# A two-layer streaming encoder on one core: the list scheduler runs twice, the second time by latest start

## The chip, the cores and the metric

The kernel runs on one core of one Trainium2 chip. The metric is device time in microseconds, the median of several executions. One execution was profiled, and every duration below is from it.

## What is computed

Two layers run over 544 frames: 512 of a new stream ("prompt") and 32 of a running one ("sample"), which also reads a cache of 512 past frames. All is fp32.

```python
h = rmsnorm(x, g_attn); z = h @ w_in
o_da = rmsnorm((softmax(q1 k1) - lam * softmax(q2 k2)) @ v) * (1 - lam_init)   # 8 heads, two softmaxes each
o_mla = latent_attention(...)                                                  # 8 heads, one softmax each
x = x + (sigmoid(gA) * o_da + sigmoid(gB) * o_mla) @ w_o
u = rmsnorm(x, g_ffn) @ w_up                                                   # 5632 columns
x = x + (silu(conv3(u)[:2816]) * conv3(u)[2816:]) @ w_down
y = rmsnorm(x, g_final)                                                        # after the second layer
```

Masks are causal by chunks of 64 frames. The outputs are y, the new cache rows and the last two rows of u.

## The kernel before, in words

**Numbers.** Each fp32 operand of a large product is split into a high part (cast to fp32r) and a low part (the rest), and a product is three matmuls: high by high, high by low, low by high. So weights come by DMA into `wf` (a ring of 2), ScalarE casts them into `wh` (ring of 3), and VectorE or GpSimd subtracts to make `wl` (ring of 3). Activations are split alike, into pages of the tile `frt`; plain fp32 pages lie in `fpt`.

**Products.** `dense` runs one block of 128 output columns over all 544 frames: per 128 rows of the weight six matmuls of 272 (or 256 and 288) frames into one of two PSUM slots, `dn`. When a block is done, VectorE evacuates the slot ("evac"). These dense matmuls are most of TensorE's work, and the program always has more of them.

**Side work.** Attention runs beside the dense products. Its score, transpose and value matmuls go into four PSUM banks, `ax`. For one head and one block of 128 queries, a score matmul fills a bank; VectorE masks it (MEMSET) and takes the row maximum (TENSOR_REDUCE `sm<-ax`); ScalarE takes the exponential into `fpt` (`softmax`); VectorE scales (`diff_norm`, `mla_norm`); TensorE transposes the result from `fpt` into an `ax` bank (`probs_t`, matmuls `ax<-ident,fpt`); ScalarE and VectorE split it, and `av` multiplies by the values. Queries and keys are rotated first (`rope_unit`): per unit four DMAs within SBUF (`fpt<-fpt`) swap groups of partitions, and GpSimd multiplies and adds. `split_rows`, `split_twice` and `sk` make high and low parts of queries, keys and cached keys. `finish` joins the two mixers of a pair of heads: per head three long VectorE operations on `fpt` and a split; its result is used only by the output product `w_o`, after all heads. `layer_consts` makes a few small vectors (`lamt`, `bh`, `gdc`).

**The order.** The kernel's code doesn't issue instructions. `Program.add` records each with the earlier ones it depends on (by tile cells, so reuse of a page or bank is a dependency too). `Program.order` then simulates the five engines: again and again it takes the engine that can start first, and on it, among the recorded instructions that are ready, the one recorded earliest. `cost` gives each instruction's time, `SIGNAL` the time from one engine's end to another's start. `emit` issues in that order, and each engine then runs its own instructions strictly in it, whatever the simulated times were. All instructions are issued from one line in `emit`: L371 before.

**Stages.** Each layer: input products with latent attention beside them, then differential attention, gates and `finish`, then `w_o` and the up- and down-products with the convolution. Layer 1 is recorded in the same way as layer 0.

## Time and profile before

| | us |
|---|---|
| median of 3 runs | 1917.09 (1914.59 to 1917.48) |
| the profiled execution, whole | 1917.5 |
| its span, first to last instruction | 1915.7 |
| TensorE busy (PE, matmuls) | 1851.4 |
| VectorE busy (DVE) | 1251.2 |
| ScalarE busy (ACT) | 878.9 |
| GpSimd busy (POOL) | 753.3 |

PE is the matmuls' engine and PEld its weight loads, which overlap; SP issues all DMAs. In the chain of work that ended last, PE has 87% and DVE 8%. A time in a row such as 330.10 is counted from the span's start. DVE instructions that share a port with POOL stretch, so one shape has several durations.

### The profile page before, as it was taken

The numbers are of one execution on the slowest core, as the hardware profiler recorded it, in microseconds if no ns is written. First come the engines' busy times: TensorE is split into PE (matmuls) and PEld (weight loads), VectorE is DVE, ScalarE is ACT, GpSimd is POOL, SyncE is SP. The second block draws the span as 40 slices with busy tenths as digits, with TensorE's granted clock in tenths as the row PEclk, the third lists the DMA queues.
The fourth block names the chain that finished last, engine by engine and source line by source line (L and its number), as shares of the span: only waits on it lengthen the run. The fifth ranks groups of instructions, "written<-read, shape, count | busy, mean of one in ns | idle before, by whom it ended". The sixth has DMA issues, their size and how long they took to land.

```text
span 1915.7 us, 37003 instructions
## 1 busy us (share of the span) xinstructions
PE 1851.4 (97%) x14244; PEld 1814.0 (95%) x14244; DVE 1251.2 (65%) x2457; ACT 878.9 (46%) x1810; POOL 753.3 (39%) x856
## 2 busy tenths in 40 slices
PE   7999999988999999999999999989899999999997
PEld 7999998988999999999999999989889999999997
DVE  6677777798747777742247677687986577777212
ACT  4455564555544444432235454654664444444322
POOL 4422636476243333312233345365653333332121
PEclk9999999999999999999999999999999999999999
DMA  4422433344352222233332225244444533333222
GB/s 154 123 79 79 142 108 117 107 141 125 95 187 88 90 90 89 89 95 117 116 121 92 92 90 157 78 144 116 124 125 128 161 89 89 89 89 88 84 88 77
DMA packets 78824, 208.40 MB, mean 109 GB/s; under 512 B 11132, under 2 KB 13880, under 8 KB 78648
## 3 DMA queue, kind: packets, MB, share of 16 engines
q1 hardware_dynamic: 78648, 206.04, 34.9%
q8 instruction: 112, 1.84, 0.4%
q14 instruction: 64, 0.52, 0.1%
HBM read 170.12 MB, written 23.62 MB: 101 GB/s over the span
## 4 chain that ended last, share of the span: by engine, by line
PE 87%; DVE 8%; issue 2%; DMA 1%; POOL 1%; ACT 1%; SPq 0%; DVEq 0%; ACTq 0%; POOLq 0%
PE dn L371 73%; PE ax L371 13%; DVE fpt L371 3%; DVE frt L371 3%; DVE sm L371 1%; POOL fpt L371 0%; DVE wl L371 0%; DMA fpt<-in_x_dram 0%; SPq L371 0%; ACT frt L371 0%; ACT fpt L371 0%; DVE ax L371 0%; DMA wf<-in_wt_dram 0%; POOL wl L371 0%; DMA fpt<-in_dk_c_dram 0%
## 5 line engine op out<-in xcount | busy, mean ns | idle before, releaser
L371 PE MATMUL dn<-frt,wh 128*128 128x272 f32 (+2 forms) x8032 | 1386.8, 291 | 12.1 <-ACT wh L371 7.2
L371 PEld LDWEIGHTS dn<-frt,wh 128*128 128x128 f32 x8032 | 1157.4, 189 | 22.0 <-ACT wh L371 7.3
L371 PE MATMUL dn<-frt,wl 128*128 128x272 f32 (+2 forms) x4000 | 849.0, 291 | 3.4 <-DVE wl L371 3.4
L371 PEld LDWEIGHTS dn<-frt,wl 128*128 128x128 f32 x4000 | 640.4, 189 | 6.7 <-DVE wl L371 3.6
L371 ACT CAST wh<-wf 128x512 fp32r<-128x512 f32 (+2 forms) x534 | 323.8, 609 | 604.3 <-PE dn L371 511.2
L371 POOL TENSOR_TENSOR wl<-wf,wh 128x512 fp32r<-128x512 f32 x242 | 320.7, 1326 | 553.5 <-ACT wh L371 533.6
L371 DVE TENSOR_TENSOR wl<-wf,wh 128x512 fp32r<-128x512 f32 (+2 forms) x290 | 211.5, 733 | 225.0 <-ACT wh L371 222.7
L371 PE MATMUL ax<-frt 128*128 128x256 f32 (+5 forms) x1164 | 228.3, 323 | 19.5 <-ACT fpt L371 12.9
L371 POOL TENSOR_TENSOR fpt<-fpt 128x544 f32<-128x544 f32 (+1 forms) x144 | 207.8, 1456 | 85.9 <-DMA fpt<-fpt 78.2
L371 DVE TENSOR_TENSOR fpt<-dn,fpt 128x544 f32<-128x544 f32 (+2 forms) x291 | 154.1, 547 | 111.0 <-PE dn L371 97.9
L371 PEld LDWEIGHTS ax<-frt 128*128 128x128 f32 (+1 forms) x1164 | 175.6, 189 | 34.8 <-ACT fpt L371 16.3
L371 DVE SCALAR_TENSOR_TENSOR fpt<-fpt,vec 128x546 f32<-128x546 f32 (+1 forms) x180 | 141.2, 785 | 47.6 <-ACT fpt L371 45.6
L371 ACT ACTIVATE fpt<-ax,sm 128x128 f32<-128x128 f32 (+4 forms) x216 | 112.3, 522 | 65.8 <-DVE sm L371 54.3
L371 ACT CAST frt<-fpt 128x544 fp32r<-128x544 f32 (+5 forms) x166 | 101.7, 622 | 50.3 <-DVE fpt L371 24.1
L371 ACT CAST frt<-ax 128x384 fp32r<-128x384 f32 (+4 forms) x186 | 71.5, 395 | 109.5 <-PE ax L371 108.6
L371 POOL COPY fpt<-cin 128x2 f32<-128x2 f32 x88 | 33.8, 384 | 202.3 <-DVE fpt L371 199.2
L371 DVE TENSOR_TENSOR frt<-fpt,frt 64x544 fp32r<-64x544 f32 (+4 forms) x120 | 99.0, 828 | 13.5 <-ACT frt L371 11.3
L371 DVE TENSOR_TENSOR frt<-ax,frt 128x384 fp32r<-128x384 f32 (+4 forms) x186 | 80.3, 446 | 37.2 <-ACT frt L371 24.7
L371 DVE TENSOR_REDUCE sm<-ax 128x1 f32<-128x128 f32 (+4 forms) x216 | 99.2, 473 | 6.7 <-PE ax L371 5.1
L371 PE MATMUL ax<-ident,fpt 128*128 128x128 f32 (+1 forms) x480 | 82.4, 279 | 18.6 <-DVE fpt L371 16.0
L371 DVE SCALAR_TENSOR_TENSOR frt<-fpt,frt 128x544 fp32r<-128x544 f32 (+1 forms) x76 | 79.1, 1040 | 24.9 <-ACT frt L371 24.0
L371 POOL CAST frt<-frt 64x32 fp32r<-64x32 f32 (+1 forms) x172 | 64.4, 378 | 55.6 <-ACT frt L371 34.6
(88 smaller groups left out, 1192.3 us busy)
## 6 DMA issues: line engine op xcount, KB each, us to landing
wf<-in_wt_dram SPq DMA_DIRECT2D x243, 512.0 KB, 3.6
fpt<-fpt SPq DMA_DIRECT2D x168, 68.0 KB, 2.7
wf<-in_wt_dram SPq DMA_DIRECT2D x16, 384.0 KB, 3.1
fpt<-in_x_dram SPq DMA_DIRECT2D x16, 272.0 KB, 3.6
out_o_dv_dram<-fpt SPq DMA_DIRECT2D x16, 272.0 KB, 2.1
out_o_dk_dram<-fpt SPq DMA_DIRECT2D x16, 272.0 KB, 4.3
xa<-fpt SPq DMA_DIRECT2D x16, 272.0 KB, 2.1
fpt<-xa SPq DMA_DIRECT2D x16, 272.0 KB, 3.6
```

Of the source, the lines that this page charges most:

```text
L371: getattr(getattr(self.nc, eng), name)(*args, **kw)
```

## The change

What is computed, the tiles, the recorded instructions and their dependencies are the same (19734 of them). Three things in the scheduler differ:

- `SIGNAL` and `cost` have other numbers; `MARGIN` (5% on each cost) is gone. `cost` now says too whether an instruction uses the port that DVE and POOL share, and the simulation lets such instructions wait for each other (`port`). `GAP` adds 18 ns behind each instruction of DVE, ACT and POOL.
- DMAs: before, SyncE was held at least 475 ns by each; now 60 ns, and the transfer takes its turn on one shared line (`dma`).
- `order` runs the simulation twice. The first run ranks by the place in the program, as before. `latest` walks that order backwards from the program's end and gives every instruction its latest start: the time at which its first user must start, less signal and cost; TensorE's instructions are also held by the one that follows on TensorE. The second run ranks ready instructions of the other engines by that latest start, and TensorE's still by the place in the program.

```diff
-MARGIN = {"vector": 1.05, "scalar": 1.05, "gpsimd": 1.05}
 SIGNAL = {e: dict(zip(ENGINES, t)) for e, t in (
-    ("tensor", (0, 230, 260, 230, 100)),
-    ("vector", (235, 127, 180, 200, 60)),
-    ("scalar", (240, 140, 0, 210, 60)),
-    ("gpsimd", (190, 90, 90, 104, 60)),
-    ("sync", (0, 0, 0, 0, 0)))}
+    ("tensor", (0, 38, 37, 64, 60)),
+    ("vector", (55, 0, 35, 64, 60)),
+    ("scalar", (100, 33, 0, 78, 60)),
+    ("gpsimd", (55, 34, 33, 0, 60)),
+    ("sync", (60, 60, 60, 60, 60)))}
+GAP = {"tensor": 0.0, "vector": 18.0, "scalar": 18.0, "gpsimd": 18.0}
+PORT_TAIL = {"vector": 100.0, "gpsimd": 150.0}
...
         if eng == "tensor":
-            if name == "transpose" or kw["rhs"].dtype != F32:
-                return max(n, 256) / 2.4 + 2.5, 0.0
-            return 2 * (max(2 * n, 256) / 2.4 + 2.5), 0.0
+            if name == "matmul" and kw["rhs"].dtype == F32:
+                return 2 * max(109.0, 0.907 * n + 1.5), False
+            part = name == "matmul" and kw["lhsT"].ap[0][1] < 128
+            return max(109.0, 0.4535 * n + 1.5) + 190 * part, False
...
+    def latest(self, order):
+
+        late = [0.0] * len(self.ops)
+        need = [0.0] * len(self.ops)
+        chain = 0.0
+        for i in reversed(order):
+            e = self.ops[i][0]
+            t = min(need[i], chain) if e == "tensor" else need[i]
+            late[i] = t = t - self.cost(i)[0]
+            if e == "tensor":
+                chain = t
+            for j in self.deps[i]:
+                f = self.ops[j][0]
+                need[j] = min(need[j], t - (0.0 if e == f and e != "sync" else SIGNAL[f][e]))
+        return late
+
     def order(self):
+        late = self.latest(self.schedule(range(len(self.ops))))
+        return self.schedule([i if op[0] == "tensor" else late[i] for i, op in enumerate(self.ops)])
+
+    def schedule(self, rank):
...
-            i = heapq.heappop(a)
-            hold, lat = self.cost(i)
-            hold *= MARGIN.get(e, 1.0)
-            self.start[i] = t
-            free[e] = t + hold
+            i = heapq.heappop(a)[1]
+            if e == "sync":
+                ap = self.ops[i][2][0]
+                free[e] = t + 60
+                dma = max(t + 1300, dma) + width(ap) * ap.ap[0][1] * 4 / 300.0
+                end = dma + 700
+            else:
+                hold, shared = self.cost(i)
+                end = (max(t, port) if shared else t) + hold
+                if shared:
+                    port = end - PORT_TAIL[e]
+                free[e] = end + GAP[e]
```

All instructions are now issued from L411 instead of L371. Three places show how they moved.

**DVE in the first layer's differential attention, at 319 to 329 us of the profile.** `SCALAR_TENSOR_TENSOR fpt<-fpt` and `fpt<-fpt,gdc` and the split behind them are `finish`; `MEMSET ax` and `TENSOR_REDUCE sm<-ax` are the softmaxes of the next heads. Before:

```order
L371 TENSOR_REDUCE sm<-ax_96 128x1
L371 SCALAR_TENSOR_TENSOR fpt<-fpt 128x544
L371 MEMSET ax_97 64x64
L371 MEMSET ax_95 64x64
L371 SCALAR_TENSOR_TENSOR fpt<-fpt,gdc 128x512
L371 SCALAR_TENSOR_TENSOR fpt<-fpt,gdc,oms 128x32
L371 SCALAR_TENSOR_TENSOR fpt<-fpt 128x544
L371 TENSOR_REDUCE sm<-ax_97 128x1
L371 SCALAR_TENSOR_TENSOR fpt<-fpt,gdc 128x512
L371 TENSOR_TENSOR frt<-fpt,frt 128x544
L371 SCALAR_TENSOR_TENSOR fpt<-fpt,gdc,oms 128x32
L371 MEMSET ax_98 64x64
```

In the changed kernel, from the same softmax on:

```order
L411 TENSOR_REDUCE sm<-ax_96 128x1
L411 MEMSET ax_97 64x64
L411 MEMSET ax_95 64x64
L411 TENSOR_REDUCE sm<-ax_95 128x1
L411 TENSOR_REDUCE sm<-ax_97 128x1
L411 RECIPROCAL rs<-sm 128x1
L411 MEMSET ax_96 64x64
L411 TENSOR_REDUCE sm<-ax_96 128x1
L411 RECIPROCAL sm<-sm 128x1
L411 TENSOR_TENSOR wl<-wf,wh 128x512
L411 TENSOR_TENSOR fpt<-dn_93,fpt 128x544
L411 MEMSET ax_95 64x64
```

The seven instructions of `finish` left this place; the first of them now stand three rows below the last one shown, behind four of the softmaxes' maxima, two weights' low parts and an evacuation.

**DVE a little later, at 408 to 416 us.** `frt<-fpt,frt 64x544` is `split_rows`, `frt<-fpt,frt 128x512` is `sk`, and `fpt<-fpt,sm` is `diff_norm`, whose result TensorE transposes. Before:

```order
L371 MEMSET ax_97 64x64
L371 SCALAR_TENSOR_TENSOR frt<-fpt,frt 64x544
L371 TENSOR_TENSOR frt<-fpt,frt 128x512
L371 RECIPROCAL sm<-sm 128x1
L371 TENSOR_REDUCE sm<-ax_97 128x1
L371 SCALAR_TENSOR_TENSOR sm<-sm,coef 128x1
L371 SCALAR_TENSOR_TENSOR frt<-fpt,frt 64x544
L371 SCALAR_TENSOR_TENSOR fpt<-fpt,sm 128x384
```

In the changed kernel:

```order
L411 RECIPROCAL sm<-sm 128x1
L411 SCALAR_TENSOR_TENSOR sm<-sm,coef 128x1
L411 SCALAR_TENSOR_TENSOR fpt<-fpt,sm 128x384
L411 TENSOR_TENSOR frt<-ax_95,frt 128x128
L411 MEMSET ax_97 64x64
L411 TENSOR_REDUCE sm<-ax_97 128x1
L411 MEMSET ax_96 64x64
L411 TENSOR_REDUCE sm<-ax_96 128x1
L411 TENSOR_TENSOR frt<-fpt,frt 128x512
```

`diff_norm` of 384 columns stood behind both `split_rows` and `sk`; now it stands ahead of all three.

**PE at 328 to 331 us**, where a score matmul of 512 keys (`ax_95<-frt 128x512`) stands among dense ones. Before:

```order
L371 MATMUL ax_97<-frt 128x384 x2
L371 MATMUL dn_93<-frt,wh 128x272 x3
L371 MATMUL dn_93<-frt,wl 128x272 x2
L371 MATMUL dn_94<-frt,wh 128x272 x4
L371 MATMUL dn_94<-frt,wl 128x272 x2
L371 MATMUL dn_94<-frt,wh 128x272 x4
L371 MATMUL dn_94<-frt,wl 128x272 x2
L371 MATMUL dn_94<-frt,wh 128x272 x4
L371 MATMUL dn_94<-frt,wl 128x272 x2
L371 MATMUL dn_94<-frt,wh 128x272 x2
L371 MATMUL ax_95<-frt 128x512 x2
```

In the changed kernel:

```order
L411 MATMUL ax_96<-frt 128x384 x2
L411 MATMUL dn_93<-frt,wl 128x272
L411 MATMUL dn_93<-frt,wh 128x272 x4
L411 MATMUL dn_93<-frt,wl 128x272 x2
L411 MATMUL dn_93<-frt,wh 128x272 x4
L411 MATMUL dn_93<-frt,wl 128x272 x2
L411 MATMUL ax_95<-frt 128x512 x2
L411 MATMUL dn_94<-frt,wh 128x272 x4
L411 MATMUL dn_94<-frt,wl 128x272 x2
L411 MATMUL dn_94<-frt,wh 128x272 x4
L411 MATMUL dn_94<-frt,wl 128x272 x2
```

The matmul of 512 keys now comes ahead of the whole next dense block (`dn_94`) instead of 20 matmuls into it, and the one of 384 keys in `ax_97`, 5 matmuls ahead of that block before, comes 38 matmuls into it. In all, 4427 of TensorE's 14178 recorded instructions stand at another place, 1436 of DVE's 2457, 665 of ACT's 1593, 290 of POOL's 852 and 242 of SyncE's 654.

## Rows read from the trace of the kernel before

**Rows 1.** Page, busy time: us, share of the span, instructions.

```profile
PE 1851.4 (97%) x14244; PEld 1814.0 (95%) x14244; DVE 1251.2 (65%) x2457; ACT 878.9 (46%) x1810; POOL 753.3 (39%) x856
```

**Rows 2.** Windows by stage: stretch, its length, busy us of each engine (instructions), granted clock, DMA.

```profile
0.00:30.00 30.00, 17.93 (x91) 16.29 (x92) 20.12 (x24) 13.97 (x22) 15.59 (x15) 0.92 0.61 192
...
300.00:480.00 180.00, 162.87 (x1219) 155.87 (x1219) 146.25 (x317) 98.21 (x235) 117.81 (x116) 0.99 0.40 124
...
1250.00:1430.00 180.00, 162.54 (x1210) 155.75 (x1210) 150.65 (x330) 100.76 (x248) 112.78 (x113) 0.99 0.43 127
...
1895.00:1916.00 21.00, 9.99 (x74) 9.28 (x72) 7.35 (x20) 2.68 (x6) 4.54 (x6) 0.84 0.30 106
```

**Rows 3.** Waits of PE in 300 to 480 us: us in total, times, longest.

```profile
PE ax L371 <- ACT fpt L371: 7.4, 7, 2.1
PE ax L371 <- DVE fpt L371: 6.9, 5, 3.2
```

**Rows 4.** Chain that ended last: start, us, what; the longest undisturbed dense stretch.

```profile
571.93 392.64 PE dn L371 x3144
```

**Rows 5.** Windows of the first burst and of the stretch behind it.

```profile
320.00:348.00 28.00, 23.11 (x170) 21.31 (x169) 27.75 (x53) 15.94 (x40) 20.86 (x21) 1.00 0.34 97
348.00:380.00 32.00, 32.00 (x241) 30.88 (x241) 21.52 (x64) 17.06 (x44) 9.98 (x9) 1.00 0.32 104
```

**Rows 6.** Timeline of DVE, 320 to 329 us: start, us, instruction.

```profile
320.07 1.87 DVE L371 SCALAR_TENSOR_TENSOR fpt<-fpt 128x544 f32<-128x544 f32 x1 [0.60 <-POOL fpt L371]
...
322.05 0.67 DVE L371 SCALAR_TENSOR_TENSOR fpt<-fpt,gdc 128x512 f32<-128x512 f32 x1
322.65 0.24 DVE L371 SCALAR_TENSOR_TENSOR fpt<-fpt,gdc,oms 128x32 f32<-128x32 f32 x1
322.81 0.71 DVE L371 SCALAR_TENSOR_TENSOR fpt<-fpt 128x544 f32<-128x544 f32 x1
...
323.65 1.55 DVE L371 SCALAR_TENSOR_TENSOR fpt<-fpt,gdc 128x512 f32<-128x512 f32 x1
325.13 1.88 DVE L371 TENSOR_TENSOR frt<-fpt,frt 128x544 fp32r<-128x544 f32 x1
326.93 1.34 DVE L371 SCALAR_TENSOR_TENSOR fpt<-fpt,gdc,oms 128x32 f32<-128x32 f32 x1
...
328.31 0.68 DVE L371 TENSOR_REDUCE sm<-ax 128x1 f32<-128x256 f32 x2
```

**Rows 7.** Timeline of PE: two of its longest waits, in brackets.

```profile
330.10 0.74 PE L371 MATMUL ax<-frt 128*128 128x512 f32 x2 [2.06 <-ACT fpt L371]
...
416.09 0.55 PE L371 MATMUL ax<-ident,fpt 128*128 128x128 f32 x3 [3.20 <-DVE fpt L371]
```

**Rows 8.** Timeline of DVE, 408 to 416 us.

```profile
408.80 1.80 DVE L371 SCALAR_TENSOR_TENSOR frt<-fpt,frt 64x544 fp32r<-64x544 f32 x1
410.63 1.75 DVE L371 TENSOR_TENSOR frt<-fpt,frt 128x512 fp32r<-128x512 f32 x1
...
413.56 1.83 DVE L371 SCALAR_TENSOR_TENSOR frt<-fpt,frt 64x544 fp32r<-64x544 f32 x1
415.42 0.62 DVE L371 SCALAR_TENSOR_TENSOR fpt<-fpt,sm 128x384 f32<-128x384 f32 x1
```

**Rows 9.** Timeline at the start: DVE, and PE's wait for a weight's low part.

```profile
15.81 1.24 DVE L371 TENSOR_TENSOR lamt<-lamv 64x2 f32<-64x2 f32 x1
19.40 1.06 DVE L371 TENSOR_SCALAR bh<-vec 128x16 f32<-128x16 f32 x1
26.52 0.82 PE L371 MATMUL dn<-frt,wl 128*128 128x272 f32 x2 [3.35 <-DVE wl L371]
```

**Rows 10.** Windows behind the waits at 468 to 473 us; the clock is third from the end.

```profile
473.00:475.00 2.00, 2.00 (x9) 1.90 (x10) 1.99 (x8) 1.51 (x5) 1.80 (x4) 0.50 0.05 18
```

**Rows 11.** Timeline of SP: the issue of two shuffles in a row.

```profile
1395.34 1.15 SPq L371 DMA_DIRECT2D fpt<-fpt  x2
```

**Rows 12.** Waits of POOL: us in total, times, longest.

```profile
POOL fpt L371 <- DMA fpt<-fpt: 78.2, 28, 6.2
```

## What the change will do to the time
> **What bounds the kernel now.** I read the page's busy times first: PE is busy 1851.4 of 1915.7 us and no other engine over 65% [rows 1]. So the end is set by the matmuls and by what keeps PE from them, 64.3 us of idle time. The undisturbed stretch in the middle of the chain shows what a dense matmul takes: 392.64 us for 3144, 124.9 ns each [rows 4]. No order can shorten that work; an order can only remove idle time.
>
> The windows by stage say where the idle time is (length less PE's busy time, [rows 2]): 12.1 us in the first 30, of which 7.2 lie before the first matmul; 17.1 in 300 to 480; 17.5 in 1250 to 1430, the same stage of layer 1; and 10.7 behind 1895 (up to the span's end at 1915.7). That leaves 64.3 less 57.4 = 6.9 for the 1500 us between. Two stages of differential attention thus hold 34.6 us.
>
> Next, who PE waits for there: ACT and DVE writing `fpt`, 14.3 of the 17.1 us [rows 3]. ACT's share is the softmax too: a score matmul needs a bank whose exponential has not run, because DVE's maximum for it was late. The windows around the first waits show DVE busy 27.75 of 28 us and, right behind, 21.52 of 32, while PE loses 4.9 us in the first and nothing in the second [rows 5]. DVE has the capacity; its work comes in bursts. The timeline shows what it does in one: from 320.07 to 328.27 stand seven instructions of `finish` [rows 6], whose result nothing uses before `w_o`. The maximum that the bank at 330.10 hangs on comes at 328.31, and PE waits 2.06 us [rows 7]. At 416.09 PE waits 3.20 us for a scaling of 384 columns that began at 415.42 [rows 7, 8]; ahead of it stood three splits of new queries and keys.
>
> **The change part by part.** Nothing is added or removed, so all costs are waits.
>
> *The two attention stages.* In the first burst the seven `finish` instructions, 1.87+0.67+0.24+0.71+1.55+1.88+1.34 = 8.26 us [rows 6], go behind the maxima. The wait they precede is 2.06 us, so it should go whole, though PE's matmul now also stands 20 matmuls earlier, 2.5 us at 124.9 ns: 8.3 less 2.5 still covers 2.06. At 416 the three splits, 1.80+1.75+1.83 = 5.38 us [rows 8], go behind the scaling; its wait is 3.20. Elsewhere the order shows the same picture: at most of PE's longer waits of these stages less DVE work stands ahead of what PE needs, or PE has more dense matmuls ahead of its question (the 384-key scores of the fence on PE come 43 matmuls later, 5.4 us). At a few (six of the 26 longest) neither moved. I take four fifths of 34.6, **28 us**; bounds 0 (DVE's work is conserved) and 34.6.
>
> What does the moved work wait for next? `finish` has until `w_o`. DVE is busy 146.25 of 180 us in the first stage and 150.65 of 180 in the second [rows 2]; shortened by 14 each, that is 88% and 91%: tight but possible.
>
> *The start.* Ahead of the low part that PE awaits for 3.35 us at 26.52, DVE ran `lamt` and `bh`, 1.24+1.06 us [rows 9], which now stand behind it. The low part keeps the sums of squares ahead of it. Of the 4.9 us that PE idles after its first matmul (12.1 less 7.2) I take **3.5**; bounds 0 and 4.9. The 7.2 before it hang on the first loads and stay.
>
> *The other stretches*, 6.9 us [rows 2]. Some waits lose DVE work, but PE's question moved up as well: a third, **2.5**; bounds 0 and 6.9. *The end*: the last instructions keep their order, so 0 of the 10.7.
>
> *The clock.* Behind the waits at 468 to 473 us the granted clock reads 0.50, the 1.2 GHz level [rows 10]; 9 matmuls ran in 2 us instead of 16 at 124.9 ns. The mean clock of each attention stage is 0.99 [rows 2], so falls cost 1% of 180 us in each, 1.8. If PE stops idling before them, they go: 3.6 us at most, 0 at least; I take **2**.
>
> *What the tighter plan costs.* The old table left 230 ns from PE to DVE, the new 38. So in many places PE asks sooner: the 512-key scores, 20 matmuls. Where that meets a late engine, a new wait appears that the trace of before can't show. Going through some twenty such places, PE's question moved up by 5 to 28 matmuls (0.6 to 3.5 us) against a slack of 0.1 to 1.5 us, which bounds new waits by 0 and 17 us. I take **8**, near the middle, since the engines that answer are now often earlier too.
>
> *Sum.* -28 -3.5 -2.5 -2 +8 = -28 us. The profiled execution took 1917.5, so **1889.5**; it is 0.4 above the median of the runs, 1917.09, which is nothing here. A measurement of this kernel can tell some 0.2% (3.8 us) from no change.
>
> **The rivals.**
>
> *DVE stays the bound (0.22).* In a burst DVE is busy all the time [rows 5], and work put off 4 us falls on the next head's. For it: 88 to 91% is a load at which something is nearly always late. Against it: the 32 us behind the burst hold 10.5 idle ones. Then half of the 28 comes back, the clock falls stay: -14-3.5-2.5+8 = -12, **1905.5**. One shape of `finish` took 1.87 us and 0.71 us in the same burst [rows 6], the long one while POOL worked. The Trainium skill (SBUF — State Buffer, "SBUF: two separate sides") says that DVE instructions with two SBUF inputs and GpSimd instructions exclude each other for a whole instruction; the two durations agree. By that rule moved work keeps its collisions, which speaks for this rival.
>
> *The score banks bind (0.10).* Waits that ACT ends are waits for an `ax` bank, 7.4 of 17.1 us in the first stage [rows 3]. If four banks are simply too few, those stay: 28 less 2 x 0.8 x 7.4 = 16; the sum is -16, **1901.5**. The Trainium skill (Perfetto Trace Analysis, "Optimization Strategy") reads bubbles that repeat on the engine that should be saturated as possibly too little SBUF or PSUM for the next tile. The trace agrees that a bank is what is waited for, but shows its reader late behind `finish`.
>
> *SyncE is underpriced: slower (0.10).* The new plan holds SyncE 60 ns per DMA. Two shuffles in a row took 1.15 us [rows 11], so the four of a rotation need 2.3, and the last leaves up to 2.1 us after the plan has it. POOL runs strictly in order; it already waited for shuffles 28 times, 78.2 us [rows 12], and weights' low parts stand behind the rotation on its queue. A layer has 21 rotations. If PE then waits 2.1 us at each of 42, that is 88 us; it breaks even with the gain of 28 at 13 of them. At half of them the time is 1917.5-28+44 = **1933.5**. Against it: PE's waits name POOL's rotations nowhere.
>
> *The new waits equal the old (0.06)*, 1917: both orders keep PE in program order, and two thirds of its instructions stand where they stood.
>
> **How the numbers follow.** The forecast's own case has 0.52: range 1871 (34.6+4.9+6.9 gone and no new wait: 46) to 1902 (new waits of 17, half of the small terms). Faster: 0.52+0.22+0.10 = 0.84, less a little for a weak form of the second, 0.82; slower by SyncE and other new waits 0.11; within 0.2%, 0.07. The range takes in the DVE and bank rivals: 1870 to 1912, leaving out slower and no change (0.18).
>
> **What would show it.** Right: PE's idle time in the two attention stages falls from 17 to some 4 to 8 us each; DVE's 99% windows thin out; `finish` runs in stretches where DVE idled; the clock falls after 400 us vanish. Wrong: PE idle there above 12 us with DVE still over 95% busy beside it (DVE rival), waits ended by ACT as large as before (bank rival), or PE waiting for POOL's low parts behind rotations (SyncE).

## The result, and the profile after

The changed kernel takes **1943.95 us** (median of 4 runs, 1940.44 to 1944.73) against 1917.28 for the kernel before, measured beside it: a ratio of **1.0132**, 95% interval 1.0103 to 1.0161. It is slower by 1.3%, where 1889.5 us had been forecast. Its profiled execution took 1943.76 us, span 1942.0.

First the busy time of PE, from the page, beside [rows 1], and the cores view of the kernel before and of the changed one (span, mean granted clock).

```profile
PE 1872.5 (96%) x14244; PEld 1832.2 (94%) x14244; DVE 1261.2 (65%) x2457; ACT 882.9 (45%) x1810; POOL 773.6 (40%) x856
```

```profile
core 0: 1915.7 us, clock 0.994
```

```profile
core 0: 1942.0 us, clock 0.980
```

The span grew by 26.3 us. Idle time of PE is span less busy: 64.3 us before, 69.5 now, so only 5.2 of the 26.3. The other 21.1 are *busy* time of the same 14244 matmuls. The clock is why: the trace's clock record has 4 stretches at 0.50 (the 1.2 GHz level) that end before PE does in the kernel before, 17.1 us together, and 14 now, 71.7 us. The time from each PE instruction's start to the next one's, less waits, less the median of the same pair of shapes, says the same: inside the stretches at 0.50 the excess is 7.8 us before and 31.7 now, everywhere else 41.9 and 37.6. So the dense matmul is what it was (124.9 ns; the longest undisturbed stretch is again 392.64 us for 3144), and some 24 us are lost at the lower level.

The windows by stage, to be held against [rows 2]:

```profile
0.00:30.00 30.00, 18.47 (x97) 16.78 (x98) 20.50 (x27) 14.27 (x22) 16.93 (x16) 0.84 0.61 195
300.00:480.00 180.00, 167.34 (x1207) 160.31 (x1206) 135.96 (x299) 91.80 (x221) 110.57 (x111) 0.95 0.36 113
1250.00:1430.00 180.00, 167.04 (x1224) 159.49 (x1223) 139.24 (x295) 93.92 (x224) 112.59 (x111) 0.96 0.39 115
```

In these two windows PE idles 12.7 us (17.1 before) and 13.0 (17.5), 8.9 less together. But a window ends at a fixed time, the changed kernel reaches the end of each attention stage later, and its last waits there (0.62, 2.64 and 0.46 us at 483 to 487, and 0.62, 2.64 and 0.71 us at 1437 to 1441) lie outside. Windows that hold the whole stage in both kernels, first before, then changed:

```profile
300.00:490.00 190.00, 172.87 (x1293) 165.65 (x1293) 155.54 (x349) 105.74 (x257) 121.10 (x119) 0.99 0.42 128
1250.00:1445.00 195.00, 177.52 (x1323) 170.19 (x1323) 162.60 (x361) 110.67 (x273) 115.42 (x116) 0.99 0.43 125
```

```profile
300.00:490.00 190.00, 173.62 (x1240) 165.78 (x1239) 145.34 (x317) 97.13 (x235) 116.79 (x117) 0.94 0.37 115
1250.00:1445.00 195.00, 178.08 (x1292) 169.79 (x1291) 153.37 (x326) 101.21 (x244) 121.14 (x120) 0.96 0.40 119
```

Counted so, PE idles 16.4 us (17.1 before) and 16.9 (17.5): 1.3 less, not 8.9. And with *more* busy time it got through *fewer* matmuls (1240 for 1293, 1292 for 1323), at a clock of 0.94 and 0.96 where 0.99 stood. Within the first stage the idle time moved: it grew from 5.3 to 7.1 us between 300 and 365 us and from 3.2 to 3.7 between 460 and 490, and fell from 8.6 to 5.5 in the stretch between.

Behind the stages there are new waits. The timeline of PE at the entry of `w_o`, layer 0, in the changed kernel:

```profile
534.96 0.77 PE L411 MATMUL dn<-frt,wh 128*128 128x272 f32 x4 [3.21 <-ACT frt L411]
536.56 0.82 PE L411 MATMUL dn<-frt,wh 128*128 128x272 f32 x2 [0.83 <-DVE frt L411]
```

The kernel before, at the same matmul:

```profile
524.39 1.28 PE L371 MATMUL dn<-frt,wh 128*128 128x272 f32 x6 [0.23 <-ACT frt L371]
```

Layer 1 repeats it at 1487.83 (3.20) and 1489.43 (0.60). The two entries cost 7.8 us of idle time, six times what the attention stages gained. What the clock does behind such a wait shows in windows of the changed kernel (length; busy us and instructions of PE, PEld, DVE, ACT, POOL; granted clock):

```profile
348.00:355.00 7.00, 5.99 (x27) 5.96 (x28) 6.84 (x10) 2.80 (x7) 3.45 (x4) 0.51 0.34 98
536.00:542.50 6.50, 5.94 (x25) 5.71 (x26) 3.58 (x8) 2.66 (x5) 2.16 (x4) 0.50 0.05 19
```

25 matmuls in 5.94 us of busy time; at 124.9 ns they need 3.1.

**What became of the first burst** [rows 5 to 7]. PE waits there 2.39 us at 333.25 and then five times in a row. PE of the changed kernel:

```profile
333.25 0.62 PE L411 MATMUL ax<-frt 128*128 128x384 f32 x2 [2.39 <-ACT fpt L411]
...
343.76 0.73 PE L411 MATMUL ax<-frt 128*128 128x512 f32 x2 [0.83 <-ACT fpt L411]
345.06 0.30 PE L411 MATMUL ax<-ident,fpt 128*128 128x128 f32 x1 [0.56 <-ACT fpt L411]
345.71 0.41 PE L411 MATMUL ax<-ident,fpt 128*128 128x128 f32 x2 [0.35 <-DVE sm L411]
346.85 0.55 PE L411 MATMUL ax<-ident,fpt 128*128 128x128 f32 x3 [0.73 <-DVE frt L411]
349.01 1.09 PE L411 MATMUL ax<-ident,fpt 128*128 128x128 f32 x4 [1.62 <-DVE sm L411]
```

DVE, POOL, ACT and SP of the same stretch (four cuts of the timeline):

```profile
332.74 3.63 DVE L411 SCALAR_TENSOR_TENSOR fpt<-fpt 128x544 f32<-128x544 f32 x2 [2.52 <-POOL fpt L411]
336.41 1.72 DVE L411 SCALAR_TENSOR_TENSOR fpt<-fpt,gdc 128x512 f32<-128x512 f32 x1
338.06 1.34 DVE L411 SCALAR_TENSOR_TENSOR fpt<-fpt,gdc,oms 128x32 f32<-128x32 f32 x1
339.33 1.90 DVE L411 SCALAR_TENSOR_TENSOR fpt<-fpt,gdc 128x512 f32<-128x512 f32 x1
341.15 1.81 DVE L411 TENSOR_TENSOR frt<-fpt,frt 128x544 fp32r<-128x544 f32 x1
...
343.11 0.42 DVE L411 TENSOR_REDUCE sm<-ax 128x1 f32<-128x256 f32 x1
```

```profile
328.28 12.40 POOL L411 TENSOR_TENSOR fpt<-fpt 128x544 f32<-128x544 f32 x8 [5.47 <-DMA fpt<-fpt]
```

```profile
332.74 0.37 ACT L411 ACTIVATE fpt<-ax,sm 128x128 f32<-128x128 f32 x1 [3.25 <-POOL fpt L411]
```

```profile
323.54 1.96 SPq L411 DMA_DIRECT2D fpt<-fpt  x2
...
327.13 2.41 SPq L411 DMA_DIRECT2D fpt<-fpt  x4
```

Read it upwards. SyncE takes 2.41 us to issue four shuffles of a rotation, 0.6 each, where the plan has 0.24 for the four. POOL has waited 5.47 us, until a shuffle of the pair issued from 323.54 on landed; the four from 327.13 on belong to the next rotation. Then POOL does eight multiplications and additions of rotations in one block of 12.40 us. ACT's exponential and DVE's first `finish` instruction stand behind a buffer of that block: ACT idles 3.25 us, DVE 2.52. So `finish` did leave the place ahead of the maxima, as the order said, and landed some 12 us later ahead of the *next* maximum (343.11): six instructions with 10.4 us of busy time. PE waits 2.39 us for ACT and 4.1 us in pieces for what stood behind `finish`. Layer 1 has the same picture: four shuffles at 1282.54 in 2.40 us, POOL waiting 4.61 us and then doing eight operations of rotations in blocks of 2.66 and 9.54 us, PE waiting 2.36 us at 1298.83.

**And of the place at 416 us** [rows 7, 8]. The scaling of 384 columns is no longer what PE waits for there. PE and DVE of the changed kernel:

```profile
415.01 1.30 PE L411 MATMUL ax<-frt 128*128 128x512 f32 x4 [1.85 <-ACT fpt L411]
...
428.96 0.33 PE L411 MATMUL ax<-frt 128*128 128x128 f32 x1 [2.49 <-ACT frt L411]
```

```profile
409.62 1.71 DVE L411 TENSOR_TENSOR frt<-fpt,frt 128x544 fp32r<-128x544 f32 x1 [1.41 <-ACT frt L411]
...
411.69 1.43 DVE L411 TENSOR_TENSOR frt<-fpt,frt 128x544 fp32r<-128x544 f32 x1
```

Two other splits, of 544 columns, stand at 409.62 and 411.69, maxima come behind them, and PE waits 1.85 us for an exponential at 415.01 and 2.49 us at 428.96. Still, this is the place that gained: the 3.20 us went, and so did waits around it, 3.1 us of idle time in all between 365 and 460 us.

### The profile page after: what moved, and what is told of

Same layout as the page of the kernel before. It is cut to its first block, busy times and chain, and to the rows that moved or that the text cites. A ratio compares the mean times of both kernels' runs of the same rounds, so it can differ in the third digit from the quotient of the medians.

```text
span 1942.0 us, 37014 instructions
## 1 busy us (share of the span) xinstructions
PE 1872.5 (96%) x14244; PEld 1832.2 (94%) x14244; DVE 1261.2 (65%) x2457; ACT 882.9 (45%) x1810; POOL 773.6 (40%) x856
## 4 chain that ended last, share of the span: by engine, by line
PE 87%; DVE 6%; DMA 2%; ACT 2%; issue 1%; POOL 1%; SPq 0%; DVEq 0%; POOLq 0%; ACTq 0%
PE dn L411 74%; PE ax L411 13%; DVE fpt L411 2%; DVE frt L411 2%; ACT frt L411 1%; POOL fpt L411 1%; DMA fpt<-fpt 1%; DVE sm L411 1%; DMA wf<-in_wt_dram 1%; SPq L411 0%; DVE wl L411 0%; ACT wh L411 0%; ACT fpt L411 0%; DMA fpt<-in_x_dram 0%; DMA fpt<-rd 0%
## 5 line engine op out<-in xcount | busy, mean ns | idle before, releaser
L411 PE MATMUL dn<-frt,wh 128*128 128x272 f32 (+2 forms) x8032 | 1395.1, 293 | 21.7 <-ACT frt L411 13.1
L411 PEld LDWEIGHTS dn<-frt,wh 128*128 128x128 f32 x8032 | 1166.0, 190 | 32.3 <-ACT frt L411 13.6
L411 PE MATMUL dn<-frt,wl 128*128 128x272 f32 (+2 forms) x4000 | 856.3, 293 | 0.3 <-DVE wl L411 0.3
L411 PEld LDWEIGHTS dn<-frt,wl 128*128 128x128 f32 x4000 | 645.9, 191 | 3.3 <-DVE wl L411 0.7
L411 ACT CAST wh<-wf 128x512 fp32r<-128x512 f32 (+2 forms) x534 | 323.5, 609 | 634.8 <-PE dn L411 584.8
L411 POOL TENSOR_TENSOR wl<-wf,wh 128x512 fp32r<-128x512 f32 x242 | 322.9, 1335 | 633.2 <-ACT wh L411 602.0
L411 DVE TENSOR_TENSOR wl<-wf,wh 128x512 fp32r<-128x512 f32 (+2 forms) x290 | 207.9, 719 | 210.0 <-ACT wh L411 206.4
L411 PE MATMUL ax<-frt 128*128 128x256 f32 (+5 forms) x1164 | 228.7, 324 | 20.8 <-ACT fpt L411 13.3
L411 DVE TENSOR_TENSOR fpt<-dn,fpt 128x544 f32<-128x544 f32 (+2 forms) x291 | 152.1, 548 | 141.8 <-PE dn L411 127.9
L411 POOL TENSOR_TENSOR fpt<-fpt 128x544 f32<-128x544 f32 (+1 forms) x144 | 204.8, 1438 | 88.7 <-DMA fpt<-fpt 82.1
L411 PEld LDWEIGHTS ax<-frt 128*128 128x128 f32 (+1 forms) x1164 | 177.8, 190 | 38.8 <-ACT fpt L411 16.6
L411 DVE SCALAR_TENSOR_TENSOR fpt<-fpt,vec 128x546 f32<-128x546 f32 (+1 forms) x180 | 141.1, 785 | 48.0 <-ACT fpt L411 44.8
L411 ACT ACTIVATE fpt<-ax,sm 128x128 f32<-128x128 f32 (+4 forms) x216 | 112.3, 523 | 88.2 <-DVE sm L411 67.8
L411 DVE TENSOR_TENSOR frt<-fpt,frt 64x544 fp32r<-64x544 f32 (+4 forms) x120 | 109.8, 915 | 24.3 <-ACT frt L411 23.0
L411 ACT CAST frt<-fpt 128x544 fp32r<-128x544 f32 (+5 forms) x166 | 101.7, 622 | 50.4 <-POOL fpt L411 16.5
L411 ACT CAST frt<-ax 128x384 fp32r<-128x384 f32 (+4 forms) x186 | 71.5, 395 | 115.8 <-PE ax L411 111.4
L411 DVE TENSOR_REDUCE sm<-ax 128x1 f32<-128x128 f32 (+4 forms) x216 | 102.7, 482 | 10.5 <-PE ax L411 4.9
L411 POOL COPY fpt<-cin 128x2 f32<-128x2 f32 x88 | 45.1, 513 | 143.7 <-DVE fpt L411 140.6
L411 DVE TENSOR_TENSOR frt<-ax,frt 128x384 fp32r<-128x384 f32 (+4 forms) x186 | 80.4, 447 | 32.8 <-ACT fpt L411 24.4
L411 PE MATMUL ax<-ident,fpt 128*128 128x128 f32 (+1 forms) x480 | 84.5, 286 | 15.3 <-DVE fpt L411 7.5
L411 DVE SCALAR_TENSOR_TENSOR frt<-fpt,frt 128x544 fp32r<-128x544 f32 (+1 forms) x76 | 88.3, 1162 | 12.8 <-ACT frt L411 11.9
L411 ACT ACTIVATE fpt<-fpt,vec 128x546 f32<-128x546 f32 x88 | 74.4, 846 | 26.5 <-DVE fpt L411 26.2
```

Source lines behind the costliest of these rows:

```text
L411: getattr(getattr(self.nc, eng), name)(*args, **kw)
```

## The experiments

Theories, as the expectations below name them. **A**: the changed numbers do it, A1 the signal times (38 ns from PE where 230 stood), A2 the costs of the instructions. **B**: the second sort does it. **C**: part of the time is the lower clock behind waits, **D** denies that. **E**: SyncE's 60 ns per DMA. **F**: the time of an order scatters anyway. **P**: the rank of POOL. All runs, with the median, the ratio to the kernel before measured beside them, PE's idle time (span less busy) and the stretches at 0.50 that end before PE does, both of the profiled execution. The line of `emit` differs with the edit (L391, L410).

| run | edit | median us | ratio, 95% interval | PE idle us | at 0.50: times, us |
|---|---|---|---|---|---|
| before | | 1914.86 to 1918.42 | 1 | 64.3 | 4, 17.1 |
| changed | | 1943.95 | 1.0132 [1.0103, 1.0161] | 69.5 | 14, 71.7 |
| e1 | new numbers, one sort | 1943.80 | 1.0140 [1.0117, 1.0163] | 74.3 | 13, 78.5 |
| e2 | old numbers, two sorts | 1924.98 | 1.0038 [1.0023, 1.0053] | 66.8 | 7, 30.7 |
| e3 | changed, DVE alone by latest start | 1924.42 | 1.0042 [1.0028, 1.0056] | 55.5 | 8, 44.4 |
| e4 | changed, 382 fillers | 1935.78 | 1.0093 [1.0072, 1.0114] | 37.5 | 3, 10.2 |
| e5 | changed, old signal times | 1928.87 | 1.0051 [1.0037, 1.0065] | 65.0 | 9, 51.2 |
| e6 | before, new signal times | 1961.44 | 1.0226 [1.0191, 1.0262] | 93.0 | 7, 37.5 |
| e7 | e2, DVE alone by latest start | 1925.97 | 1.0043 [1.0024, 1.0062] | 64.1 | 8, 27.3 |
| e8 | changed, 155 fillers | 1934.98 | 1.0077 [1.0050, 1.0103] | 52.6 | 9, 47.8 |
| e9 | changed, 575 ns per DMA on SyncE | 1929.39 | 1.0063 [1.0046, 1.0081] | 61.7 | 10, 47.8 |
| e10 | before, 100 ns more signal time | 1928.96 | 1.0074 [1.0047, 1.0100] | 72.8 | 11, 58.0 |
| e11 | e3 and e5 together | 1932.26 | 1.0080 [1.0053, 1.0107] | 66.7 | 12, 75.1 |
| e12 | changed, SyncE by program place | 1940.72 | 1.0128 [1.0106, 1.0150] | 70.9 | 15, 71.7 |
| e13 | changed, DVE and ACT by latest start | 1922.57 | 1.0033 [1.0024, 1.0042] | 60.0 | 10, 37.5 |
| e14 | before, 66 fillers | 1917.73 | 1.0003 [0.9993, 1.0013] | 56.1 | 5, 20.5 |
| n1 | before, 4% margin | 1919.57 | 1.0022 [1.0010, 1.0035] | 65.4 | 3, 13.7 |
| n2 | before, 6% margin | 1918.04 | 1.0018 [1.0008, 1.0029] | 63.9 | 8, 27.3 |
| n3 | changed, 22 ns gap | 1953.02 | 1.0201 [1.0181, 1.0221] | 76.7 | 12, 75.1 |
| n4 | e3, 22 ns gap | 1921.65 | 1.0031 [1.0016, 1.0046] | 58.1 | 9, 41.0 |

### The two halves of the change, each alone (e1, e2)

```diff
     def order(self):
-        late = self.latest(self.schedule(range(len(self.ops))))
-        return self.schedule([i if op[0] == "tensor" else late[i] for i, op in enumerate(self.ops)])
+        return self.schedule(range(len(self.ops)))
```

> The changed kernel's new numbers (costs, signal times, gaps, shared port, 60 ns hold of SyncE), but the first sort alone: every engine takes the ready piece that is first in program order, as before the change. Theory A (the numbers do it: signal times of 38 to 64 ns where 230 stood leave no slack, so PE asks before the others answer): as slow as the changed kernel or slower, 1935 to 1955 us, with ten or more stretches in which the granted clock reads 0.50. Theory B (the second sort does it: what is put off to its latest start is late at the next junction, above all at the entry of w_o of each layer): near the kernel before or under it, 1900 to 1922 us, at most six stretches at 0.50, and no wait of over 1 us at the entry of w_o (535 and 1488 us in the changed kernel's trace).

Then the other half: the second sort, with `SIGNAL`, `cost` and `MARGIN` of the kernel before and SyncE held as there.

> The second sort with the costs, signal times (230 ns from PE) and 5% margins of the kernel before. Theory A (numbers): 1890 to 1917 us, since the slack is back and the second sort still moves finish behind the maxima. Theory B (second sort): slower than before, 1930 to 1950 us, with waits of PE of over 2 us at the entry of w_o in both layers.

Measured: 1943.80 and 1924.98. The numbers alone give the whole loss, 27 us; the second sort on top of them gives nothing (1943.95), and alone it loses 8. Theory A holds for the loss; e2's time lies between the ranges of both theories. Neither half alone makes the waits of 3.2 us at the entry of `w_o`: the longest there is 1.81 and 1.79 us in the two layers of e1, and 0.93 and 0.79 in e2.

The second sort was forecast to *gain* some 36 us before the cost of the tighter plan, and where it stands alone nothing of that is there: in the windows of the whole attention stages PE of e2 idles 34.5 us, 34.6 in the kernel before. In e1 the longest wait of the burst is larger than any in the attention stages before; PE's timeline:

```profile
340.74 0.45 PE L410 MATMUL ax<-ident,fpt 128*128 128x128 f32 x1 [5.57 <-ACT fpt L410]
```

In e2 `finish` moved only behind the first maxima. PE, then DVE, then ACT of e2:

```profile
333.96 0.45 PE L391 MATMUL ax<-ident,fpt 128*128 128x128 f32 x1 [4.06 <-ACT frt L391]
```

```profile
324.56 1.87 DVE L391 SCALAR_TENSOR_TENSOR fpt<-fpt 128x544 f32<-128x544 f32 x1
...
326.49 1.63 DVE L391 SCALAR_TENSOR_TENSOR fpt<-fpt,gdc 128x512 f32<-128x512 f32 x1
328.05 1.88 DVE L391 SCALAR_TENSOR_TENSOR fpt<-fpt 128x544 f32<-128x544 f32 x1
...
329.99 1.67 DVE L391 SCALAR_TENSOR_TENSOR fpt<-fpt,gdc 128x512 f32<-128x512 f32 x1
331.59 0.41 DVE L391 TENSOR_REDUCE sm<-ax 128x1 f32<-128x256 f32 x1
```

```profile
332.03 0.47 ACT L391 ACTIVATE fpt<-ax,sm 128x256 f32<-128x256 f32 x1 [5.69 <-DVE sm L391]
```

The maximum of 256 keys at 331.59 stands behind four long `finish` instructions, ACT idles 5.69 us for it, and the longest wait of PE in the burst is 4.06 us where it was 2.06 before [rows 7]. The wait was handed on to the next softmax, and grew.

### Which of the new numbers (e5, e6, e9, e10)

e5 puts the old `SIGNAL` table into the changed kernel; e6 puts the new one into the kernel before.

```diff
-    ("tensor", (0, 230, 260, 230, 100)),
-    ("vector", (235, 127, 180, 200, 60)),
...
+    ("tensor", (0, 38, 37, 64, 60)),
+    ("vector", (55, 0, 35, 64, 60)),
...
```

> The changed kernel (two sorts, new costs) with the signal times of the kernel before back in its table (230 ns from PE where 38 and 64 stand). Theory A1 (of the new numbers it is the signal times: without that slack PE asks early everywhere): the time falls from 1944 to 1918 to 1930 us, near the second sort with all the old numbers (1925). Theory A2 (it is the new costs, such as 124.9 ns for a dense matmul where the plan had 115.8, and the shared port): 1938 to 1950 us.

> The kernel before (one sort, its costs and 5% margins) with the changed kernel's signal times alone. Theory A1: most of the 27 us that the new numbers cost without the second sort (1943.8 against 1916.9) appear here: 1932 to 1945 us. Theory A2: 1913 to 1922 us.

1928.87 and 1961.44: A1, and in e6 more than the range given. The other new numbers (costs, gap, port, SyncE) were not run alone; e5 and e2, both with two sorts and the old signal times, differ by them and lie 4 us apart. The signal times alone cost the kernel before 43 us (1961.44 less 1918.42), more than all the new numbers together (27), so with one sort the other new numbers give some of it back. Waits of PE over the whole of e6 (us in total, times, longest):

```profile
PE ax L371 <- DVE fpt L371: 28.4, 24, 3.3
PE ax L371 <- DVE frt L371: 20.9, 26, 1.3
PE dn L371 <- DVE frt L371: 8.1, 5, 2.8
PE ax L371 <- ACT fpt L371: 7.7, 11, 1.0
```

In the kernel before, the first two read 16.0 us in 14 waits and 5.3 in 6. Fifty waits of about a microsecond: PE asks everywhere a little too soon. That the clock is not the main part of this loss shows too. The profiled execution, the slowest of e6's four, has a span 50.1 us longer than the kernel before: 28.7 us more idle time and 21.4 more busy time, while the time at 0.50 went only from 17.1 to 37.5 us.

Yet the new table is the truer one. In the trace of the kernel before I took every instruction that idled and whose last producer ran on another engine, and the time from that producer's end to its start: the median is 38 ns from PE to DVE (246 cases), 37 from PE to ACT (484), 55 from DVE to PE (30), 33 from ACT to DVE (358). These are the new numbers; most of the 230 ns of the old table was slack. Not every pair fits: from DVE to POOL it is 130 ns, where the new table has 64 and the old 200.

e10 asks for more of it.

```diff
-    ("tensor", (0, 230, 260, 230, 100)),
+    ("tensor", (0, 330, 360, 330, 200)),
...
```

> The kernel before (one sort, its costs) with 100 ns more in each signal time between two engines. Theory A1, if slack helps beyond what was there: 1900 to 1913 us. If the table before already stood near its best: 1914 to 1924 us. If slack costs more than it saves from there on: over 1925 us.

1928.96, worse by 0.74%: of the three tables tried the old one is the best, and slack beyond it costs (PE idles 72.8 us). e9 restores a hold of SyncE in the changed kernel.

```diff
-                free[e] = t + 60
+                free[e] = t + 575
```

> The changed kernel, but its plan holds SyncE 575 ns for each DMA in place of 60, as two shuffles in a row took 1.15 us on SyncE in both traces. Theory E (rotations bunch because the plan thinks that SyncE issues four shuffles in 0.24 us; in the changed kernel's trace POOL waits 5.47 us for a shuffle at 328 us, then does eight additions of rotations in a row, and ACT and PE wait behind them): the time falls from 1944 to 1920 to 1932 us. Theory A1 alone (the slack of the signal times): within 6 us of 1944.

1929.39, as E expected: 14.6 us come back. In the burst PE then waits 2.4 us between 300 and 360 us (1.42, 0.64 and 0.30), against 6.5 in the changed kernel, and POOL's rotations come in blocks of three. POOL still waits 5.36 us for a shuffle there, though, so what exactly the longer hold mends in the whole program isn't shown. The waits at the entry of `w_o` are still there, 3.20 us in both layers.

### Whose rank (e3, e7, e11, e12, e13)

```diff
-        return self.schedule([i if op[0] == "tensor" else late[i] for i, op in enumerate(self.ops)])
+        return self.schedule([late[i] if op[0] == "vector" else i for i, op in enumerate(self.ops)])
```

> The changed kernel, but in the second sort DVE alone is ranked by the latest start; ACT, POOL and SyncE take the ready piece that is first in program order, as before. Theory A (numbers): 1935 to 1950 us, as the changed kernel. Theory B in the form that the chain of ACT, POOL and SyncE behind finish is what comes late: the waits at 535 and 1488 us fall under 1 us each and the time is 1895 to 1922 us. Theory B in the form that DVE's own putting off is enough to be late: the waits at 535 and 1488 us stay over 2 us, 1935 to 1950 us.

1924.42, 19.5 us faster than the changed kernel, just over the range of B's first form. (The profiled execution was the fastest of ten, 1916.56.) But the waits that I named, at the entry of `w_o`, haven't moved; PE of e3:

```profile
519.38 1.27 PE L411 MATMUL dn<-frt,wh 128*128 128x272 f32 x4 [3.21 <-ACT frt L411]
520.99 0.82 PE L411 MATMUL dn<-frt,wh 128*128 128x272 f32 x2 [0.33 <-DVE frt L411]
```

With the new numbers DVE's rank is enough to make these. What went is PE's waiting for ACT's exponentials: 15.7 us in 14 waits in the changed kernel, 1.2 in 2 here. Part of it came back at other matmuls on `ax`, as waits that ACT's writes of `frt` ended: 3.7 us in 5 waits there, 10.2 in 9 here. In sum PE's idle time is 8.8 us under that of the kernel before, but its busy time is 7.9 us over it, with 44.4 us at 0.50.

> The second sort with the numbers of the kernel before, as in the run with two sorts and old numbers (1925), but with DVE alone ranked by its latest start. If ranking ACT, POOL and SyncE is what costs (with the new numbers that was 1944 against 1924), the time falls to 1895 to 1915 us. If the new numbers cost the 20 us only together with those ranks, and DVE's own rank gains nothing: 1917 to 1930 us.

1925.97, the same as with all ranks (1924.98). With the old numbers it makes no difference whether DVE alone or every engine is ranked.

> The changed kernel, but SyncE takes the ready DMA that is first in program order in the second sort; DVE, ACT and POOL are ranked by the latest start. It splits the 20 us that DVE's rank alone gave. If it is SyncE (weights' loads and shuffles issued as late as the plan thinks possible): 1920 to 1932 us. If it is ACT and POOL: 1937 to 1948 us.

> The changed kernel with DVE and ACT ranked by their latest start in the second sort, POOL and SyncE by the place in the program. DVE alone gave 1924, all but SyncE 1941. Theory P (it is POOL: its rotations are put off to their latest start, come in one block behind late shuffles, and ACT and DVE queue up behind them): 1917 to 1930 us. If it is ACT (weights' high parts and splits put off): 1936 to 1948 us.

1940.72 with SyncE by program place, 1922.57 with POOL by program place as well. So with the new numbers and DVE ranked it is **POOL's** latest start that costs 18 us, as theory P expected. POOL of e13 in the burst:

```profile
324.98 4.85 POOL L411 TENSOR_TENSOR fpt<-fpt 128x544 f32<-128x544 f32 x3 [3.00 <-DMA fpt<-fpt]
...
335.94 4.54 POOL L411 TENSOR_TENSOR fpt<-fpt 128x544 f32<-128x544 f32 x3 [2.70 <-DMA fpt<-fpt]
```

Blocks of three in place of eight, with weights' low parts between them. PE still waits 2.58 us at 332.93 for ACT, but the five waits behind it are gone: that is the only one over 0.6 us from 315 to 350. That such bursts make up the whole 18 us isn't shown.

The idle time of PE in the two whole attention stages (300 to 490 and 1250 to 1445 us) puts the runs in order: 34.6 us before, 38.7 with the new numbers and one sort (e1), 21.2 with DVE ranked on top of that (e3), 25.0 with ACT too (e13), 33.3 with POOL too (e12), 33.3 in the changed kernel. So the second sort has a gain with the new numbers, DVE's, and POOL's rank takes most of it back. That fits a changed kernel that comes out where e1 does.

> The changed kernel with the signal times of the kernel before, and in the second sort DVE alone ranked by its latest start. If the two remedies add up (old signal times gave -15 us, DVE's rank alone -20): 1904 to 1916 us. If both mend the same waits: 1918 to 1930 us.

1932.26: the two remedies, 15 and 20 us, give 12 together. This missed both expectations, and why the two do not add up stays open.

### The clock by itself (e4, e8, e14)

Matmuls of zeros, added into an open dense group ahead of PE's instructions that wait (`FILL` gives how many ahead of which):

```diff
             for i in order:
                 eng, name, args, kw = self.ops[i]
+                if i in count:
+                    out = list(live.values())[-1]
+                    for _ in range(count[i]):
+                        self.nc.tensor.matmul(out, lhsT=self.zero[:, :128], rhs=self.zero[:, :width(out)], start=False, stop=False)
                 getattr(getattr(self.nc, eng), name)(*args, **kw)
```

> The changed kernel with 382 more matmuls on PE, of a tile of zeros into dense groups that are open there, ahead of the 43 of PE's instructions that waited over 0.3 us in the changed kernel's trace, as many as the wait is long at full clock (some 44 us in all); they add zero to the sums. One more memset on POOL. Theory C (the extra time is matmuls at the granted clock of 0.50, the 1.2 GHz level, behind waits that lie close together: some 72 us in 14 stretches against 17 in 4 before, so some 27 us): the stretches at 0.50 fall to six or fewer, the waits turn into busy time, and the time falls to 1917 to 1930 us although nothing is waited for less. Rival D (the waits themselves are the extra time, the clock follows something else): 1940 to 1955 us, with ten or more stretches at 0.50 left.

> As the run with fillers, with 155 of them in place of 382: about half of each wait, and only at the 16 longest of PE's waits (some 19 us of zero matmuls that lie inside waits, so they should not push anything). Theory C (time at the granted clock of 0.50 costs the changed kernel some 20 us beyond its waits): at most 7 stretches at 0.50 before PE's end, under 40 us in all, and 1922 to 1932 us. Rival D (the clock costs little, since it is low where PE would wait anyway): the stretches become fewer, but the time stays within 1936 to 1948 us.

e4's busy time:

```profile
PE 1897.6 (98%) x14626; PEld 1859.9 (96%) x14626; DVE 1259.3 (65%) x2457; ACT 883.4 (46%) x1810; POOL 780.5 (40%) x857
```

Three stretches at 0.50 are left of 14, 10.2 us, as C expected, and the mean clock is 0.995. 382 fillers at 124.9 ns are 47.7 us; without them PE's busy time is 1849.9, that of the kernel before (1851.4) and 22.6 under the changed one's. That is C's size for the clock, by another way. But the time fell by only 8, outside the ranges of both C and D: idle time fell by 32.0, so 47.7 us of fillers pushed the rest back by 15.7. Fewer of them (e8, 155) took 9 us off, between the two ranges; its profiled execution, the slowest of five, has 47.8 us at 0.50 and a mean clock of 0.985, the other four read 0.990 and 0.991. So the lower clock is some 21 to 24 of the 26.3 us in the *sum*, but it can't be had back by keeping PE busy at this price, and the waits it follows remain the cause.

> The kernel before with 66 zero matmuls inside seven of its waits (those over 2 us, and those ahead of its stretches at 0.50 at 25, 472 and 1360 us), about half of each wait; one more memset on POOL. Theory C (a us less at 0.50 gave 0.1 to 0.4 us in the two runs with fillers): three of the four stretches go, 13.6 us of 17.1, so 1910 to 1915 us, below both kernels. Rival D (fillers cost what the clock gives): 1916 to 1922 us.

1917.73, no change. Of the stretches at 25, 472 and 1360 us two are gone and one is shorter, but three others stand at 262, 327 and 1416 us; at 328.27 PE now waits 3.02 us. PE idles 8.2 us less, which is just what 66 fillers take. Rival D holds here; there was nothing to get back.

### How much an order scatters (n1 to n4)

```diff
-MARGIN = {"vector": 1.05, "scalar": 1.05, "gpsimd": 1.05}
+MARGIN = {"vector": 1.04, "scalar": 1.04, "gpsimd": 1.04}
```

> The kernel before with 4% margin on the costs of DVE, ACT and POOL in place of 5%: another order of equal quality by every rule named so far. Theory F (the time of an order scatters by several us however small the edit, and the order before lies at the good end of that): 1920 to 1935 us. Rival (orders of equal quality agree, so the 8 us of the second sort with old numbers are its own): 1913 to 1920 us.

> The kernel before with 6% margin. As the run with 4%: theory F 1920 to 1935 us, the rival 1913 to 1920 us.

n3 and n4 set `GAP` from 18 to 22 ns in the changed kernel and in e3.

> The changed kernel with 22 ns between two instructions of an engine in its plan in place of 18. If the loss is the changed numbers' own (signal times, SyncE): 1936 to 1952 us. If the changed order was only unlucky within the scatter of theory F: 1915 to 1935 us.

> The run in which DVE alone is ranked by its latest start (1924), with 22 ns in place of 18. If that rank mends what the new numbers do: 1917 to 1932 us. If 1924 was the scatter: 1935 to 1952 us.

Both neighbours of the kernel before stay under theory F's range, but by the ratio they are 0.2% slower, clear of 1: its order lies 3 to 5 us on the good side. The changed kernel stays slow and by 9 us slower still; the repaired one stays at 1921.65. The 27 us and the 20 us stand. Of the second sort's 8 us with old numbers only what is over some 4 can be called its own. No neighbour of e5, e9, e11, e12 or e13 was run, and the 9 us say how far an order of the changed kernel can move by itself: of their 15 to 18 us about half may be that. No version here is faster than the kernel before; of those with a second sort, DVE ranked alone (1.0031 in n4) and DVE and ACT ranked (1.0033) come nearest.

## Why the prediction was wrong

*The attention stages, -28.* The step that failed first. Both moves that I read in the order happened; "the wait they precede should go whole" did not follow. At 330 us `finish` runs later and ahead of the next maximum; in e2, where nothing else changed, the burst's longest wait went from 2.06 us to 4.06. I took a work item off one place and counted the wait there as gone, without looking for the softmax that it would now stand before. The shares of 88 and 91% that I had worked out for DVE were a warning that I gave to a rival. Over the whole stages idle time fell by 1.3 us in place of 28, and by 0.1 in e2. The place at 416 did gain, 3.1 us; the first burst lost 1.8. The mechanism isn't empty: DVE's rank on the new numbers, with POOL in program order (e3), leaves 21.2 us there, 13.4 less than before. The sum had no term for POOL's rank, which takes most of that back.

*"`finish` has until `w_o`."* True, and the plan uses it up: at `w_o` PE waits 3.21 and 0.83 us in layer 0 and 3.20 and 0.60 in layer 1, where 0.23 stood in layer 0. No term of the sum held a wait there.

*The price of a moved `finish`.* Six moved instructions took 10.4 us beside POOL's block of 12.40 us; at the entry of `w_o`, with POOL all but idle, six of the same shapes took 3.9. The Trainium skill (SBUF — State Buffer, "SBUF: two separate sides") says that DVE instructions with two SBUF inputs and GpSimd instructions that read SBUF exclude each other. The trace agrees, and I gave that rule too little weight: moving work next to POOL's longest block is what the new order did there.

```profile
531.96 0.72 DVE L411 SCALAR_TENSOR_TENSOR fpt<-fpt 128x544 f32<-128x544 f32 x1
532.72 0.75 DVE L411 SCALAR_TENSOR_TENSOR fpt<-fpt,gdc 128x512 f32<-128x512 f32 x1
```

*The start, -3.5.* DVE's wait fell from 3.35 [rows 9] to 0.35 us, as forecast, and ACT's high part took its place: 3.69 us at 21.38. Idle in the first 30 us went from 12.1 to 11.5, and the clock there from 0.92 to 0.84.

*Other stretches, -2.5.* Of the wrong sign. From 30 to 300 us idle time was 2.7 before and is 2.6 now, but from 490 to 1250 and from 1445 to 1895 us together it went from 4.2 to 11.4, and the entries of `w_o` make that up. *The end, 0:* right, 1.5 and 1.8 us as before.

*The clock, -2.* Mis-sized and of the wrong sign: +21 to +24. I priced two falls that might go and none that might come. A wait priced at its own length is too cheap where it brings a stretch at 0.50.

*The tighter plan, +8 (0 to 17).* The term that the loss hangs on, mis-sized beyond its bound: the new numbers alone cost 27 us, the signal times alone 43. I counted PE's question at some twenty places. The table has an entry for every pair of engines, and with the new ones PE has fifty waits of about a microsecond in e6.

*The rivals.* SyncE underpriced had the right sign and, with 1933.5, the nearest time, at a chance of 0.10. That nearness is luck: its sum sets 44 us of waits against a gain of 28, and neither came. Its term is real (e9: 14.6 us), but PE waits for no low part of POOL's; in the burst it is ACT and DVE that stand behind a block of rotations. DVE as the bound was right as a mechanism, as the first step shows, and by itself left a gain that didn't come. Its sign came half: PE idles over 12 us in each stage, but DVE beside the first burst is busy 12.96 of 14 us (332 to 346), not over 95%. The sign of the bank rival came too, as waits that ACT ends stayed (6.8 us from 300 to 480, 7.4 before). But e3 has the same four banks and waits 1.2 us for exponentials in the whole program, so their number is not what sets these waits.

## What to carry to other kernels

A planner's number that is truer can make a slower kernel: with 230 ns for a signal that takes 38 this kernel was at its fastest, with 38 it lost 43 us and with 330 it lost 12. What the slack was covering isn't shown; instructions of one shape that take 0.72 or 1.8 us are a candidate. Where a change has two halves, forecast each alone, and for every piece of work that is put off name the instruction it will stand in front of next; on an in-order queue there always is one. Count idle time over the whole of a stage in both kernels, not in one pair of fixed windows: the later kernel's last waits fall out of them. And price a wait with what the clock does behind it, not by its length alone.

## What the runs showed of the hardware

- Nearly the same idle time can come with very different clocks. 64.3 us of idle time came with 17.1 us at 0.50 before, 69.5 with 71.7 after. The single wait of 3.20 us at 416.09 [rows 7] had no stretch at 0.50 behind it, as a window of the kernel before shows; 3.21 us at 534.96 in the changed kernel had one of 6.8 us, from 535.9, with a further wait of 0.83 us across its start. Length alone doesn't decide it: in the kernel before, 3.05 us at 1358.48 had a stretch of 3.4 us behind it, from 1359.9. What decides it isn't shown.

```profile
410.00:425.00 15.00, 11.80 (x96) 11.53 (x95) 14.79 (x29) 10.32 (x24) 10.84 (x13) 1.00 0.49 149
```

- Not every stretch at 0.50 follows a wait: in the kernel before, the one at 1202.9 has no wait of PE over 0.15 us in the 11 us ahead of it; 32 matmuls of 32 columns stand there, 3.65 us together.
- With waits filled by matmuls of zeros the mean granted clock was 0.995 (e4), where 0.980 stood.
- `SCALAR_TENSOR_TENSOR fpt<-fpt` of 128x544 on DVE took 0.70 to 0.73 us all 14 times that POOL was idle beside it, in both traces; beside POOL it took 1.81 to 1.90 us 8 times of 18, and 0.71 to 0.74 else.
- From a producer's end to the start of what waits for it: 33 to 55 ns (median) between PE, DVE and ACT, 78 from ACT and 130 from DVE to POOL.
